# Operands of a merged projection built earlier, a gate scale moved, DMAs of two chains pinned to source order, and a reordered tail

## The chip, the cores and the metric

The kernel runs on one core of one Trainium2 chip. The metric is the time of one execution on the device in microseconds (us), the median of three runs. All arithmetic is in fp32; products on TensorE take operands that are split into a high part (fp32r) and the rest.

## The reference

One layer of an encoder is applied to two groups of 512 tokens (`g` = 0 and 1) with shared weights, model width 1024:

```python
h = rmsnorm(x, g_mix); u = h @ w_in
qk, v, o, gates, c_q, c_kv, k_r, gm = split(u)
# A: bidirectional mLSTM, 4 heads (conv + silu on qk, exponential gates, both directions added)
hm = rmsnorm(mlstm(...), g_mhead)
y_m = (sigmoid(o) * hm) @ w_mo
# B: latent attention, 8 heads, full softmax, rotary part shared
y_a = mla_attention(...) @ w_ao
g_m, g_a = sigmoid(gm)
x = x + (g_m * y_m + g_a * y_a) @ w_out
x = x + (silu(h2 @ w_gate) * (h2 @ w_up)) @ w_down      # h2 = rmsnorm(x, g_ffn)
x = x + sigmoid(x @ w_ple_gate) * (p @ w_ple)
y = rmsnorm(x, g_final)
```

## The kernel before

Activations lie transposed: a tile is 128 channels by 512 tokens of one group. `split` makes a pair of tiles for each operand: ScalarE casts the high part, VectorE subtracts it from the source for the low part. One product of two split operands is three matmuls (high by high, high by low, low by high), each 128x128 by 512 columns.

**Stages, in order.** Input norm and early projections; for each of 4 mLSTM heads its projections (`mlstm_proj`) and, for each group, `mlstm_chain`; projections of the merge gates (`merge_gate`, 16 of them, 10 before attention and the others behind attention heads 0, 1 and 3 as `BULK` says); attention, 8 heads by 2 groups, with `attn(hd, g, ...)` followed by the projections of the next head, `attn_proj(hd + 1, g, ...)`; a first chain of merged products, `w_mo` and then `w_ao`; `out_proj`; the products of the per-layer embedding (`emb`); a second chain of merged products, gate and up, then down; the gated embedding and the final norm.

**Merged products.** `chain` works through "quads". A quad covers two output column blocks by both token groups, and does with seven products (`P1`, `P2`, `P7`, `P6`, `P5`, `Q4`, `P3`) what would take eight. With an inner width of 4 tiles a product is 12 matmuls. The operand side of a quad is `Ops`: from four raw quarters, a and b (first half of the channels of group 0 and 1) and c and d (second half), it makes sums and splits them. `P1` is a, `P2` is c, `P7` is b-d, `P6` is b-d-a, `P5` is a-b, `Q4` is b-d-a+c, `P3` is d. One set of operands serves four quads. The weight side is `Seven`: when it is made it loads two 512 KB weight tiles (`wst`; two slots in the pool WP and two in WX, so two quads at a time), and before each product GpSimd adds blocks of them (for `P7`, `P6` and `P3`) and the result is split into one of five buffers `wp`. `chain` writes the products of neighbouring quads interleaved: `P6` of quad q, `P1` of q+1, `P5` of q, `P2` of q+1, `Q4` of q, `P7` of q+1, `P3` of q. Before a product it asks for the operands of that one and the next four (`need`), and makes the `Seven` of the next product's quad.

**What sets the order.** Each engine runs its queue in order. The queues are made by a scheduler with a timing model: an instruction may be moved ahead of others of its engine if the model finds it ready, and the program's order is only the priority. `tc.keep_in_program_order(r)` ties an instruction behind the one traced just before it on its engine. While `pinned[0]` is true, instructions of VectorE, ScalarE, TensorE and GpSimd are so tied (in `emb` and in the tail). DMAs, all issued from SyncE's queue (SP), are never tied before the change.

**The steps around the change.**

- mLSTM: `to` is tanh(o/2); at the end of `mlstm_chain` `zt = (to + 1) * hm` is stored to `hzd`. The factor `hg` (half of `g_mhead`, one column of 128 values for each block) is applied later in `hraw`, when the 16 tiles of `hzd` are loaded as raw quarters of `w_mo`'s operands.
- In attention head 7 (`hd == AH - 1`), the pool QL is closed, X2 (16 tiles) is opened, and `hops.need` is asked for `P1`, `P2` and `P7`, which loads all of `hzd`. `H` holds 32 tiles "h"; they hold the normalised input until the last merge gate, behind head 3.
- In the first chain, outputs of `w_mo` go through `put_z` (load a gate tile from `tmd`, multiply, store to `z1d`), those of `w_ao` through `put_y` (load from `z1d` and `tad`).
- In the second chain, the last output of each up quad makes GpSimd compute four sums and stores seven tiles to `actd`; the down quads load them back (`Loaded`).
- `emb` makes 16 products of 6 matmuls with four weight blocks `wple`, each split when its first product comes.
- The tail (pinned) works on the last two columns of group 1 in halves of 256 tokens, then sums squares, takes the inverse root, spreads it over partitions and writes the outputs (`finish`).

Of the kernel before, what the change touches and what calls it, by code (L numbers as in the profile page):

```python
# [15 lines left out]
P = 128  # L16
# [46 lines left out]
def encoder_kernel(ctx: ExitStack, tc: tile.TileContext, a):  # L63
# [3 lines left out]
    class Engine:  # L67
# [5 lines left out]
        def __getattr__(self, name):  # L73
            f = getattr(self.e, name)

            def call(*args, **kw):
                r = f(*args, **kw)  # L77
                if pinned[0]:
                    tc.keep_in_program_order(r)
                return r  # L80

            return call

    V, S, E, GP = (Engine(e) for e in (nc.vector, nc.scalar, nc.tensor, nc.gpsimd))

# [49 lines left out]
    nc.sync.dma_start(cols, a["cols"])  # L135
# [25 lines left out]
    def weight(src):  # L161
        n = src.shape[-1]
        st = WP("wst", "wst", F32, (P, 1024))
        nc.sync.dma_start(st[:, :n], src)
# [140 lines left out]
    for k in range(KD):  # L305
        nc.sync.dma_start(xs[0][k], a["x0"][k])
        if k == 0:
            wg = w8("gate")
    nc.sync.dma_start(ident, a["ident"])
# [9 lines left out]
    for k in range(KD):  # L319
        nc.sync.dma_start(xs[1][k], a["x1"][k])  # L320
# [15 lines left out]
    for g in range(G):  # L336
        s = EV("ch", "gsb")
        V.tensor_tensor(out=s, in0=early["gate", g], in1=rs1[g], op=ALU.mult)
        S.activation(out=s, in_=s, func=AF.Identity, bias=col("b_gate"))
        for d in range(2):  # L340
            for i in range(2):
                lo = 64 + 32 * i + 4 * d
                nc.sync.dma_start(rid[i][8 * d + 4 * g : 8 * d + 4 * g + 4], s[lo : lo + 4])
        nc.sync.dma_start(gsd[g], s[0:64])
# [15 lines left out]
    nc.sync.dma_start(esel, a["esel"])  # L360

    masks = []
    for d in range(2):
        st = R("tr", "mst")
        nc.sync.dma_start(st[:, 0:P], a["mask"][d])
# [11 lines left out]
    nc.sync.dma_start(lf, rid[1].rearrange("r (c t) -> (r c) t", c=8))  # L377
# [12 lines left out]
    nc.sync.dma_start(lfd.rearrange("r (c t) -> (r c) t", c=8), lf)  # L390
# [3 lines left out]
    for t, r in ((ri_n, rid[0]), (rf_n, lfd)):  # L394
        GP.memset(t, 0.0)
        for d in range(2):
            nc.sync.dma_start(t[32 * d : 32 * d + 8], r[8 * d : 8 * d + 8])
# [64 lines left out]
    def mlstm_proj(hd):  # L462
# [59 lines left out]
        for c in range(2):  # L522
            w = w8(f"o{2 * hd + c}")
            for g in range(G):
                to[g][c] = hproj(w, g, M1("to", "to"))
                S.activation(out=to[g][c], in_=to[g][c], func=AF.Tanh, scale=0.5)
        mst[hd] = (sts, va, to)

    def mlstm_chain(hd, g):
# [67 lines left out]
        for c in range(2):  # L597
# [4 lines left out]
            V.scalar_tensor_tensor(out=zt, in0=to[g][c], scalar=1.0, in1=tp, op0=ALU.add, op1=ALU.mult)  # L602
            nc.sync.dma_start(hzd[g][2 * hd + c], zt)
# [36 lines left out]
    def merge_gate(name, dst, c):  # L640
        w = w8(f"{name}{c}")
        for g in range(G):
            t = hproj(w, g, EV("bk", "tg"))
            S.activation(out=t, in_=t, func=AF.Tanh, scale=0.5)
            nc.sync.dma_start(dst[g][c], t)
# [20 lines left out]
    for half in range(2):  # L666
        whi, wlo = weight(a["wv"][half])
        for g in range(G):
            for i in range(NB):
# [9 lines left out]
                nc.sync.dma_start(vd[g][half][i], t)  # L679
    ozd = [[dr.tile([P, T], F32, name=f"ozd{g}_{c}") for c in range(AH)] for g in range(G)]  # L680
    cos = Q.pool.tile([P, T], F32, name="cos")
    nc.sync.dma_start(cos, a["cos"])
    sin = Q.pool.tile([P, T], F32, name="sin")
    nc.sync.dma_start(sin, a["sin"])
# [15 lines left out]
    for g in range(G):  # L700
        gs = Q("tr", "gs")
        nc.sync.dma_start(gs[0:64], gsd[g])
# [11 lines left out]
    def attn_proj(hd, g, wa):  # L714
# [13 lines left out]
        nc.sync.dma_start(vt.rearrange("p (a b) -> p a b", a=NB), vd[g][hd // 4].rearrange("a p c -> p a c")[:, :, c : c + P])  # L728
# [3 lines left out]
    def attn(hd, g, ops):  # L732
# [36 lines left out]
        nc.sync.dma_start(ozd[g][hd], o)  # L769

    def load(src, sl=EV, tag="bk", n="ld"):
        t = sl(tag, n)
        nc.sync.dma_start(t, src)
# [10 lines left out]
    class Ops:  # L784
# [12 lines left out]
        def part(self, name, k):  # L797
# [3 lines left out]
            if name == "P7":  # L801
                t = self.t[k] = self.tmp()
# [38 lines left out]
    class Seven:  # L841


        def __init__(self, srcs, kh, ops, out):
            n = kh * P
            st = []
            for sl, src in zip((WP, WX), srcs):
                t = sl("wst", "wst", F32, (P, 1024))
                nc.sync.dma_start(t[:, : 2 * n], src)
                st += [t[:, 0:n], t[:, n : 2 * n]]  # L850
            self.st, self.n, self.kh, self.ops, self.out = st, n, kh, ops, out
            self.bk = {}
# [23 lines left out]
        def product(self, name):  # L876
# [7 lines left out]
            for k in range(self.kh):  # L884
# [51 lines left out]
    def load4(src):  # L936
        t = ev4("ld")
        nc.sync.dma_start(t, src)
# [15 lines left out]
    for hd in range(AH):  # L954
        if hd < AH - 1:
            wa = weight(a["wa"][hd + 1])
        else:
            QL.close()
            X2 = Slots("X2", "right", x=16)
            for n in ("P1", "P2", "P7"):  # L960
                hops.need(n)
        for g in range(G):
            attn(hd, g, ops[g])
            if hd < AH - 1:
                ops[g] = attn_proj(hd + 1, g, wa)
        for _ in range(BULK[2 + hd]):
# [10 lines left out]
    def put_z(c):  # L977
        def put(at, t):
# [3 lines left out]
            nc.sync.dma_start(z1d[g][cc], m)  # L982
# [72 lines left out]
    for c in range(KD):  # L1055
# [9 lines left out]
        if c == 5:  # L1065
            st = [sl_("wst", "wst", F32, (P, 1024)) for sl_ in (WX, WX)]
            for i in range(2):
                nc.sync.dma_start(st[i], a["wple"][i])
# [7 lines left out]
    def emb(n):  # L1076
        for _ in range(n):
            c, g = todo.pop(0)
            if c // 2 == len(wple):
# [4 lines left out]
            nc.sync.dma_start(emd[g][c], t)  # L1084
# [29 lines left out]
    def gate_up(f1, f2):  # L1114
# [6 lines left out]
        def up(at, t):  # L1121
# [3 lines left out]
            if len(ac) == 4:  # L1125
# [6 lines left out]
                for n, t_ in zip(NAMES, (a_, c_, t3, t2, t1, t4, d_)):  # L1132
                    actd[f1, n] = dr.tile([P, T], F32, name=nm("actd"))
                    nc.sync.dma_start(actd[f1, n], t_)
# [70 lines left out]
    def halves(c):  # L1205
        st = (WP, WX)[c % 2]("wst", "wst", F32, (P, 1024))
        nc.sync.dma_start(st, a["w8"][W8[f"pg{c}"]])
# [23 lines left out]
    def finish(g, cs, b0=0, nb=NB):  # L1231
# [3 lines left out]
        for c0 in range(cs[0], cs[-1] + 1, per):  # L1235
# [7 lines left out]
            nc.sync.dma_start(  # L1243
# [65 lines left out]
LEAD = 2  # L1309
LATN = (3, 0)  # L1310
# [94 lines left out]
```

## Time and profile before

| | |
|---|---|
| median of 3 runs | 1937.29 us (1936.48 to 1938.13) |
| profiled execution, its own time | 1939.74 us |
| its span in the profile | 1938.0 us |
| mean granted TensorE clock in it | 0.981 |
| TensorE matmul busy | 1861.9 us, 96% |
| VectorE busy | 1260.3 us, 65% |
| ScalarE busy | 874.7 us, 45% |
| GpSimd busy | 474.4 us, 24% |
| moved by DMA | 203.40 MB, mean 105 GB/s |

Engines in the profile: PE is TensorE's matmul, PEld its weight load, DVE VectorE, ACT ScalarE, POOL GpSimd, SP the queue of DMA issues. Times are from the start of the span. A row of the timeline reads: start, duration, engine, line, operation, tile written <- tiles read, form, count, and in brackets the idle time of the engine before it with what ended it. The wrapper around the engines records every operation, so all of them carry its line (L77), and they are told apart by their tiles: `b` and `mm` are products, `wp` weight splits, `xh` and `xl` the two parts of an operand of a merged product, `sc`, `pt` and `av` the three steps of attention. A row of the windows view reads: stretch, its length, busy time and count of PE, PEld, DVE, ACT and POOL, granted clock, DMA share, GB/s.

### The profile page before, as it was taken

The numbers are of one execution on the slowest core, as the hardware profiler recorded it, in microseconds if no ns is written. First come the engines' busy times: TensorE is split into PE (matmuls) and PEld (weight loads), VectorE is DVE, ScalarE is ACT, GpSimd is POOL, SyncE is SP. The second block draws the span as 40 slices with busy tenths as digits, with TensorE's granted clock in tenths as the row PEclk, the third lists the DMA queues.
The fourth block names the chain that finished last, engine by engine and source line by source line (L and its number), as shares of the span: only waits on it lengthen the run. The fifth ranks groups of instructions, "written<-read, shape, count | busy, mean of one in ns | idle before, by whom it ended". The sixth has DMA issues, their size and how long they took to land. (4 is left out here: it accounts for less than half of the span.)

```text
span 1938.0 us, 24531 instructions
## 1 busy us (share of the span) xinstructions
PE 1861.9 (96%) x8836; PEld 1542.6 (80%) x8836; DVE 1260.3 (65%) x2135; ACT 874.7 (45%) x1711; POOL 474.4 (24%) x349
## 2 busy tenths in 40 slices
PE   7999999999999999979899989999999999999997
PEld 6888898988888888758777867777887777788886
DVE  7657575746455676878996667445444458778757
ACT  5245454535354566784533435233333344434442
POOL 3000000100000001234630014565466654232100
PEclk9999999999999999989999989999999999999998
DMA  4110112012262122137554331233223346534232
GB/s 161 50 44 33 55 35 64 34 60 82 82 202 90 55 74 73 53 115 239 163 200 153 109 114 66 87 111 106 94 97 102 115 135 218 163 120 142 87 125 87
DMA packets 95578, 203.40 MB, mean 105 GB/s; under 512 B 10400, under 2 KB 21024, under 8 KB 95456
## 3 DMA queue, kind: packets, MB, share of 16 engines
q1 hardware_dynamic: 95456, 201.83, 31.2%
q8 instruction: 69, 1.13, 0.2%
q14 instruction: 53, 0.43, 0.1%
HBM read 147.69 MB, written 54.10 MB: 104 GB/s over the span
## 5 line engine op out<-in xcount | busy, mean ns | idle before, releaser
L77 PE MATMUL b<-xh,wp 128*128 128x512 f32 x2296 | 723.4, 396 | 17.9 <-ACT wp L77 8.3
L77 PEld LDWEIGHTS b<-xh,wp 128*128 128x128 f32 x2296 | 434.5, 190 | 124.4 <-ACT wp L77 11.7
L77 PE MATMUL b<-xl,wp 128*128 128x512 f32 x1148 | 452.4, 394 | 5.9 <-DVE xl L77 5.7
L77 DVE TENSOR_TENSOR wp<-wst,wp 128x512 fp32r<-128x512 f32 (+1 forms) x284 | 271.9, 964 | 108.8 <-ACT wp L77 108.0
L77 ACT CAST wp<-wst 128x512 fp32r<-128x512 f32 (+1 forms) x284 | 171.0, 611 | 345.4 <-PE b L77 228.1
L77 PEld LDWEIGHTS b<-xl,wp 128*128 128x128 f32 x1148 | 217.8, 190 | 54.3 <-DVE xl L77 7.6
L77 PE MATMUL mm<-hh,whi 128*128 128x512 f32 x592 | 233.1, 394 | 7.2 <-ACT whi L77 7.0
L77 PE MATMUL mm<-hh,wlo 128*128 128x512 f32 x592 | 232.4, 394 | 2.2 <-DVE wlo L77 2.2
L77 PE MATMUL mm<-hl,whi 128*128 128x512 f32 x592 | 233.0, 394 | 1.1 <-DVE hl L77 1.1
L77 POOL TENSOR_TENSOR s<-wst,wst 128x512 f32<-128x512 f32 (+1 forms) x42 | 61.6, 1466 | 449.5 <-DMA wst<-w 323.4
L77 PEld LDWEIGHTS mm<-hh,whi 128*128 128x128 f32 x592 | 112.2, 190 | 30.6 <-ACT whi L77 7.0
L77 POOL TENSOR_TENSOR wst<-wst 128x512 f32<-128x512 f32 (+1 forms) x84 | 125.7, 1496 | 35.3 <-DVE wp L77 30.7
L77 PEld LDWEIGHTS mm<-hh,wlo 128*128 128x128 f32 x592 | 112.1, 189 | 26.1 <-DVE wlo L77 3.4
L77 PEld LDWEIGHTS mm<-hl,whi 128*128 128x128 f32 x592 | 112.1, 189 | 25.5 <-DVE hl L77 2.3
L77 DVE TENSOR_TENSOR u<-b,u 128x512 f32<-128x512 f32 x90 | 61.3, 687 | 107.6 <-PE b L77 82.7
L77 ACT CAST whi<-wst 128x1024 fp32r<-128x1024 f32 (+1 forms) x71 | 73.1, 1029 | 110.4 <-PE mm L77 77.6
L77 DVE TENSOR_TENSOR wlo<-wst,whi 128x1024 fp32r<-128x1024 f32 (+1 forms) x71 | 86.0, 1211 | 28.7 <-ACT whi L77 28.3
L77 POOL TENSOR_TENSOR vnl<-avt,vnh 128x512 fp32r<-128x512 f32 x16 | 21.5, 1345 | 317.6 <-ACT vnh L77 284.6
L77 DVE TENSOR_TENSOR xl<-ld,xh 128x512 fp32r<-128x512 f32 x109 | 88.7, 846 | 8.1 <-ACT xh L77 7.8
L77 PE MATMUL mm<-xh,wp 128*128 128x512 f32 (+1 forms) x288 | 81.7, 368 | 0.0
L77 ACT COPY u<-b 128x512 f32<-128x512 f32 x90 | 50.9, 586 | 66.6 <-PE b L77 65.6
L77 DVE TENSOR_TENSOR x<-x,b 128x512 f32<-128x512 f32 x84 | 56.9, 682 | 32.8 <-PE b L77 32.4
(269 smaller groups left out, 3379.4 us busy)
## 6 DMA issues: line engine op xcount, KB each, us to landing
wst<-w SPq DMA_DIRECT2D x135, 512.0 KB
ld<-actd SPq DMA_DIRECT2D x77, 256.0 KB
actd<-t SPq DMA_DIRECT2D x44, 256.0 KB
actd<-sg SPq DMA_DIRECT2D x33, 256.0 KB
x<-x SPq DMA_DIRECT2D x32, 256.0 KB
wst<-wd SPq DMA_DIRECT2D x16, 512.0 KB
hzd<-hz SPq DMA_DIRECT2D x16, 256.0 KB
tmd<-tg SPq DMA_DIRECT2D x16, 256.0 KB
```

The lines of the kernel that those rows point to most:

```text
L77: r = f(*args, **kw)
```

## The change

1. **Gate scale.** `to` becomes `hg * tanh + hg` with one more ScalarE operation for each of 16 tiles in `mlstm_proj`; the product at the end of `mlstm_chain` loses its `+ 1`, and `hraw` loses its 16 scaling operations.
2. **Operands earlier.** For heads 4 and 5 (`HOPS`), behind each of the four (head, group) steps, one of the four k of `P1`, `P2`, `P7` and `P6` is built: 4 loads into a small stage of 4 tiles, 4 splits, one subtraction on VectorE and one on GpSimd, both in place. At head 7 nothing is built; the raw quarters are forgotten, and `P5`, `Q4` and `P3` load all 16 quarters again, into X2, inside the chain. `Q4` is made from the quarters with two subtractions where there was one addition.
3. **Queue.** Inside `chain`, each DMA is tied behind the one traced before it. The `Seven` of quads 0 and 1 is made right at their first product; that of quad q+2 right behind the matmuls of `P3` of quad q and ahead of its outputs (the `hook`).
4. **`emb`.** A block of `wple` is split one block (four products) ahead.
5. **Tail.** The last column of the last half (`embed(KD - 1, ...)`) is moved ahead of two of the four output tiles of the first half, its square is kept apart (`keep=True`, so the sum takes two operands), and the other outputs are spread over the waits that follow.

```diff
+    queued = [False]
+
+    def dma(out, in_):
+        r = nc.sync.dma_start(out, in_)
+        if queued[0]:
+            tc.keep_in_program_order(r)
...  (every nc.sync.dma_start becomes dma)
@@ mlstm_proj
                 S.activation(out=to[g][c], in_=to[g][c], func=AF.Tanh, scale=0.5)
+                hc = hg[:, 2 * hd + c : 2 * hd + c + 1]
+                S.activation(out=to[g][c], in_=to[g][c], func=AF.Identity, scale=hc, bias=hc)
@@ mlstm_chain
-            V.scalar_tensor_tensor(out=zt, in0=to[g][c], scalar=1.0, in1=tp, op0=ALU.add, op1=ALU.mult)
+            V.tensor_tensor(out=zt, in0=to[g][c], in1=tp, op=ALU.mult)
@@ Ops.part
-                t = self.t[k] = self.tmp()
+                t = self.t[k] = self.tmp() or self.get("b", k)
                 add(out=t, in0=self.get("b", k), in1=self.get("d", k), op=ALU.subtract)
...
-            else:
+            elif k in self.t:
                 t = self.t[k]
                 add(out=t, in0=t, in1=self.get("c", k), op=ALU.add)
+            else:
+                t = self.get("c", k)
+                add(out=t, in0=t, in1=self.get("a", k), op=ALU.subtract)
+                add(out=t, in0=t, in1=self.get("d", k), op=ALU.subtract)
@@ Seven.product
+            if name == "P3" and self.hook:
+                self.hook()
             self.out(name, self.bk)
@@ chain
+        queued[0] = True
+
+        def make(i):
+            if i < len(quads) and i not in made:
+                made[i] = quads[i][1]()
+
         for at, (q, n) in enumerate(order):
             for i, m in order[at : at + look + 1]:
                 quads[i][0].need(m)
-            for i, m in order[at : at + 2]:
-                if i not in made:
-                    made[i] = quads[i][1]()
+            make(q)
+            if n == "P3":
+                made[q].hook = lambda q=q: make(q + 2)
             made[q].product(n)
+        queued[0] = False
@@ operands of w_mo
+    stage = [(H, "rs"), (H, "rs"), (EV, "bk"), (EV, "bk")]
+    raws = [0]
+
     def hraw(g, k):
-        t = load(hzd[g][k], X2, "x")
-        S.activation(out=t, in_=t, func=AF.Copy, scale=hg[:, k : k + 1])
-        return t
-
-    tmps = [(H, "rs"), (H, "rs"), (EV, "bk"), (EV, "bk")]
-    hops = Ops(hraw, lambda: (lambda s: s[0](s[1], "t"))(tmps.pop(0)), lambda n: V if n == "P7" else GP)
+        raws[0] += 1
+        return load(hzd[g][k], *stage[raws[0] % 4])
+
+    hops = Ops(hraw, None, lambda n: V if n == "P7" else GP)
+    hops.tmp = lambda: None
@@ attention
             X2 = Slots("X2", "right", x=16)
-            for n in ("P1", "P2", "P7"):
-                hops.need(n)
+            hops.r, hops.t = {}, {}
+            hops.raw = lambda g, k: load(hzd[g][k], X2, "x")
         for g in range(G):
             attn(hd, g, ops[g])
             if hd < AH - 1:
                 ops[g] = attn_proj(hd + 1, g, wa)
+            if hd in HOPS:
+                for n in ("P1", "P2", "P7", "P6"):
+                    hops.need(n, [2 * HOPS.index(hd) + g])
@@ emb
-            if c // 2 == len(wple):
+            while len(wple) < min(4, c // 2 + 2):
@@ tail
-    finish(1, [0, 1, 2, 3], 0, H0)
-    embed(KD - 1, 1, bk[3], toks[1], bps[1])
+    first = rs2[1]
+    finish(1, [0, 1], 0, H0)
+    embed(KD - 1, 1, bk[3], toks[1], bps[1], True)
+    finish(1, [2, 3], 0, H0)
     sums(1, H0, H0)
     inv(1, H0)
-    rs_ = rs2[1]
+    finish(1, [4, 5], 0, H0)
     spread3(1, H0, H0)
-    rs2[1], rs_ = rs_, rs2[1]
-    finish(1, [4, 5, 6, 7], 0, H0)
-    rs2[1] = rs_
+    rs2[1], second = first, rs2[1]
+    finish(1, [6, 7], 0, H0)
+    rs2[1] = second
...
+HOPS = (4, 5)
```

More of the change, by code (lines that the diff above doesn't have):

```diff
@@ L134, in encoder_kernel @@
     cols = cp.tile([P, NCOL], F32, name="cols")
-    nc.sync.dma_start(cols, a["cols"])
+    dma(cols, a["cols"])
     ident = cp.tile([P, P], F32, name="ident")
@@ L701, in encoder_kernel @@
         gs = Q("tr", "gs")
[L702 removed]
+        dma(gs[0:64], gsd[g])
         r = rope(gs, 2)
@@ L768, in attn @@
         S.copy(o, ob)
-        nc.sync.dma_start(ozd[g][hd], o)
+        dma(ozd[g][hd], o)
     def load(src, sl=EV, tag="bk", n="ld"):
         t = sl(tag, n)
-        nc.sync.dma_start(t, src)
+        dma(t, src)
         return t
@@ L981, in put @@
             V.scalar_tensor_tensor(out=m, in0=m, scalar=1.0, in1=t, op0=ALU.add, op1=ALU.mult)
-            nc.sync.dma_start(z1d[g][cc], m)
+            dma(z1d[g][cc], m)
         return put
@@ L1083, in emb @@
             S.copy(t, proj1(wple[c // 2], pp[g], 2, (c % 2) * 256))
-            nc.sync.dma_start(emd[g][c], t)
+            dma(emd[g][c], t)
     emb(2)
@@ L1133, in up @@
                     actd[f1, n] = dr.tile([P, T], F32, name=nm("actd"))
-                    nc.sync.dma_start(actd[f1, n], t_)
+                    dma(actd[f1, n], t_)
         def make(kind, put):
```

51 lines of the change are left out of this document (26 added, 25 removed).

## The prediction

> **What bounds the kernel now.** I read the page first (shares of the engines, slices), then the waits of PE, then the windows view over those stretches where PE is not full, and last the timelines of SP, ACT and PE at the places that the change touches.
>
> ```profile
> PE 1861.9 (96%) x8836; PEld 1542.6 (80%) x8836; DVE 1260.3 (65%) x2135; ACT 874.7 (45%) x1711; POOL 474.4 (24%) x349
> PE   7999999999999999979899989999999999999997
> PEclk9999999999999999989999989999999999999998
> ```
>
> PE is the bound nearly everywhere. What a change can win lies in the few slices that show 7 or 8, and these are also the ones where the granted clock falls. The waits of PE say who ends the larger stalls:
>
> ```profile
> PE sc L77 <- ACT p L77: 9.8, 4, 3.6
> PE b L77 <- ACT wp L77: 8.3, 4, 4.5
> PE b L77 <- DVE xl L77: 5.7, 3, 5.3
> ```
>
> The first is attention (`sc`), the second late weights of merged products, the third late operands of merged products. By stage:
>
> ```profile
> 100.00:540.00 440.00, 439.65 (x2563) 389.35 (x2562) 267.39 (x609) 211.37 (x519) 17.35 (x30) 1.00 0.17 57
> ...
> 756.00:785.40 29.40, 29.32 (x149) 23.75 (x147) 22.91 (x50) 22.19 (x47) 8.71 (x7) 1.00 0.16 54
> 785.40:814.10 28.70, 26.19 (x129) 20.97 (x128) 24.72 (x55) 21.39 (x44) 5.45 (x5) 1.00 0.18 56
> 814.10:839.00 24.90, 24.72 (x126) 20.46 (x124) 17.88 (x42) 21.49 (x47) 4.70 (x4) 1.00 0.44 153
> 839.00:871.50 32.50, 18.34 (x64) 13.19 (x65) 24.62 (x42) 26.21 (x52) 11.84 (x8) 0.74 0.18 62
> 871.50:900.00 28.50, 28.50 (x127) 23.42 (x126) 23.96 (x29) 14.53 (x27) 13.52 (x9) 1.00 0.88 294
> ...
> 1133.00:1144.00 11.00, 10.70 (x54) 8.40 (x52) 4.89 (x15) 5.08 (x9) 1.30 (x1) 1.00 0.54 193
> 1144.00:1166.00 22.00, 16.03 (x49) 11.78 (x49) 20.35 (x28) 12.44 (x23) 8.83 (x6) 0.77 0.33 120
> ```
>
> The mLSTM (first row) leaves PE no idle time. Heads 4, 5, 6 and 7 are the next four rows: the last one issues 64 PE instructions in 32.5 us where head 6 issues 126 in 24.9. The first merged chain starts full (127 in 28.5 us, so 0.224 us for one matmul and 2.7 us for a product of 12). `emb` loses half of its second stretch.
>
> **The price of a stall** is more than its length:
>
> ```profile
> 964.62 0.80 PE L77 MATMUL b<-xl,wp 128*128 128x512 f32 x1 [5.34 <-DVE xl L77]
> ...
> 962.70:969.70 7.00, 5.08 (x12) 4.07 (x13) 7.00 (x7) 3.28 (x6) 6.92 (x5) 0.51 0.62 198
> ...
> 1231.02 0.50 PE L77 MATMUL b<-xh,wp 128*128 128x512 f32 x1 [1.92 <-ACT wp L77]
> ...
> 1232.00:1236.00 4.00, 3.75 (x9) 2.95 (x10) 3.57 (x4) 1.11 (x2) 3.23 (x3) 0.57 0.00 0
> ```
>
> A 5.34 us stall was followed by 5.1 us at a clock of 0.51, 12 matmuls in place of 23: 2.5 us more. A stall of 1.92 us cost a stretch at 0.57 too, some 1.7 us more. I add 2.5 and 1.7. [...]
>
> **Part 1 and 2a, head 7.** What stands there now:
>
> ```profile
> L77 ACT ACTIVATE ld<-ld,hg 128x512 f32<-128x512 f32 x16 | 11.5, 753 | 0.0
> L77 ACT CAST xh<-ld 128x512 fp32r<-128x512 f32 x8 | 4.9, 649 | 0.0
> ...
> L77 DVE TENSOR_TENSOR xl<-t,xh 128x512 fp32r<-128x512 f32 x8 | 8.5, 1084 | 2.4 <-ACT xh L77 2.3
> L77 DVE TENSOR_TENSOR xl<-ld,xh 128x512 fp32r<-128x512 f32 x8 | 5.8, 740 | 1.4 <-ACT xh L77 1.3
> ```
>
> These lie ahead of attention's own casts and exponentials on ACT (26.2 busy of 32.5). At head 6's rate (24.9/126 = 0.198 us) 64 instructions take 12.7 us, so 19.8 are lost. The change takes all of it away. The 16 scalings go to the mLSTM: 16 x 0.75 = 12 us of ACT where it has 211 of 440 busy and PE waits for nothing; without that cover they would cost up to 12. I take 0.
>
> The 16 splits, 4 subtractions on DVE and 4 on POOL go to heads 4 and 5. There DVE has 22.9 + 24.7 = 47.6 us busy in 58.1, and gets 16 x 0.74 + 4 x 0.69 = 14.6: 62.2, over the span. ACT gets 16 x 0.65 = 10.4 onto 43.6 and stays below. Head 6 has 7 us of DVE to spare, into which the last quarter can slide. So heads 4 and 5 turn from PE-bound to DVE-bound, at about +4. Head 7 alone, with no projections to lay beside its softmax, keeps some loss; the row nearest to it is head 5's (129 instructions, 25.5 at 0.198, in 28.7: 3.2), and I take 4. Heads: -19.8 + 4 + 4 = -12. Ends: -18 (nothing lost in 4 and 5) and -3 (stalls there that bring the half clock along).
>
> **Part 2b and 3a, the opening of the first chain.** This is the dear part.
>
> ```profile
> 777.79 0.33 SPq L849 DMA_DIRECT2D wst<-w  x1
> ...
> 871.36 0.40 PE L77 MATMUL b<-xh,wp 128*128 128x512 f32 x1
> ...
> 871.56 0.59 ACT L77 COPY oz<-av 128x512 f32<-128x512 f32 x1 [1.20 <-PE av L77]
> ...
> 872.44 0.38 SPq L769 DMA_DIRECT2D ozd<-oz  x1
> ...
> 907.68 0.38 SPq L849 DMA_DIRECT2D wst<-w  x1
> ...
> 911.12 0.62 ACT L77 CAST wp<-wst 128x512 fp32r<-128x512 f32 x1 [0.51 <-DMA wst<-w]
> ```
>
> Now the last weight tile of quads 0 and 1 is loaded 90 us ahead (777.79), and the first merged matmul (871.36) follows the last of attention without a gap. Tied to source order, that load stands behind the store of the last head, which waits for the last `av` matmul. PE has nothing else left. The gap: copy 0.59, store issued 0.38, load to cast 911.12 - 907.68 = 3.44, cast 0.62: 5.0, with the clock 7.5.
>
> Then `P1` of quad 1. Ahead of its load SP has eight reloads for `P5`, a gate tile, the first `z1d` store, and eight reloads for `Q4`. The store can go once `P2` is out and multiplied: 5.0 + 2.5 + 2 x 2.7 + about 1.4 = 14.3 us after attention. Eight reloads are 2.1 MB, at 294 GB/s (windows row) 7.1 us, then 0.5 MB (1.8), about 1 to start and the cast: 24.8. `P1` is due at 7.5 + 4 x 2.7 = 18.3: 6.5 late. Sum 14. Ends: 7.5 (the scheduler lays `P5` and `P3` of quad 0 into that hole) and 22: `Q4` now has eight POOL additions, and beside POOL a DVE split took 1.08 in place of 0.74, so that `Q4` of quad 0 is late next. [...]
>
> **Part 3b, the rest of the first chain.** Weights of quads 2 to 5 stand behind the `z1d` store of `Q4` two products before.
>
> ```profile
> 909.96 1.29 DVE L77 TENSOR_TENSOR u<-b,u 128x512 f32<-128x512 f32 x2 [3.71 <-PE b L77]
> ...
> 914.68 1.52 SPq L982 DMA_DIRECT2D z1d<-ld  x2
> ```
>
> Two outputs taken from PSUM at 909.96 were stored 4.7 and 5.9 us later. The load has to go 3.44 + 0.62 = 4.1 us ahead of `P1`, which stands 5.4 us (`P3`, `P6`) behind the start of `P3`: a store later than 4.1 us after `Q4` (2.7 + 1.4) stalls PE. I take +3, one or two small stalls in four quads, since those stores were late with nothing waiting for them. Ends 0 and +22 (below).
>
> **Part 3c, gate, up and down.** Here the tie is meant to work, and a row shows what it can win:
>
> ```profile
> 1224.45 1.68 SPq L1134 DMA_DIRECT2D actd<-t  x2
> 1226.23 0.38 SPq L849 DMA_DIRECT2D wst<-w  x1
> ...
> 1230.34 0.62 ACT L77 CAST wp<-wst 128x512 fp32r<-128x512 f32 x1 [8.26 <-DMA wst<-w]
> ```
>
> A weight load stood behind `actd` stores on SP, ACT waited 8.26 us, and PE 1.92. With the hook the weights go ahead of the stores. The wait `b <- ACT wp` holds 8.3 us in four stalls, with the clock about 14. Some of them may hang on DVE's or ACT's own order: -9, ends 0 and -14. Past the hook, loads for down stand behind seven stores; other products cover them.
>
> **Part 4, `emb`, and the opening of the second chain.**
>
> ```profile
> 1145.38 0.50 PE L77 MATMUL mm<-plh,wp 128*128 128x512 f32 x1 [1.24 <-ACT wp L77]
> ...
> 1147.27 0.80 PE L77 MATMUL mm<-plh,wp 128*128 128x512 f32 x1 [1.16 <-DVE wp L77]
> ...
> 1156.36 0.50 PE L77 MATMUL mm<-plh,wp 128*128 128x512 f32 x1 [2.28 <-ACT wp L77]
> ...
> 1158.38 0.80 PE L77 MATMUL mm<-plh,wp 128*128 128x512 f32 x1 [1.29 <-DVE wp L77]
> ...
> 1165.64 1.84 SPq L1084 DMA_DIRECT2D emd<-em  x2
> ...
> 1166.19 0.39 PE L77 MATMUL b<-xh,wp 128*128 128x512 f32 x1
> ```
>
> All four stalls are the splits that now come one block ahead: 49 instructions at 0.224 are 11.0 of the 22 us: -11, ends -6 (the stalls alone) and -11. But the first weights of the next chain are then tied behind the last `emd` store, as in the first: 5.0 and the clock, +7.5, where PE now goes on at 1166.19 without a gap. Ends +5 and +9.
>
> **Part 5, the tail.**
>
> ```profile
> 1923.56 1.65 DVE L77 SCALAR_TENSOR_TENSOR o<-x,cols,rbc 128x256 f32<-128x256 f32 x4
> ```
>
> Two of these four outputs now come behind the last column (0.8) and the sum of squares on DVE (0.4) goes; two more small matmuls on PE come: -1, ends -2 and 0. The rest of the outputs stays on DVE.
>
> **The sum**: -12 + 14 + 3 - 9 - 11 + 7.5 - 1 = -8.5 against the profiled span of 1938.0: 1929.5. That execution's own time is 1939.74, 2.45 above the median of the runs, so the median becomes 1937.29 - 8.5 = 1928.8.
>
> **Rivals.**
> - *Slower: `z1d` stores hold the weights.* Place: quads 2 to 5 of the first chain. With a store 8 us after `Q4` each load is 3.9 late, with the clock 5.6, four times: 22 in place of 3, and 1928.8 + 19 = 1948. It decides from a total of 15, a store some 6 us late. For it: the 5.9 above. Against: DVE put splits ahead of those multiplications because nothing waited.
> - *Heads 4 and 5 do not absorb.* Three steps in four stall long enough for the half clock: heads -3 in place of -12, 1937.8. For it: DVE at 62 of 58. Against: the work is spread over four steps and free to slide.
> - *The tie does not do what it says.* The late `wp` casts stay, because ACT's order has them behind other waits: 0 in place of -9, 1937.8. For it: 8.26 us is one wait of an in-order queue. Against: a DMA ended it.
>
> **How the numbers follow.** No change is within 0.2%, 3.9 us. Chances: the forecast 0.50 (its own range 1916 to 1934), slower 0.25, heads 0.15, no tie 0.10. The two middle cases fall mostly within 3.9 us of before. Faster 0.53: nearly all of the first and a part of the last two; same 0.21; slower 0.26. The range, 1909 to 1946, takes the good ends of heads and queue together below and most of the slower rival above.
>
> **What would show it.** No `ld<-ld,hg` on ACT, and head 7 near 17 us; DVE near full between 756 and 815; a PE gap of about 5 us ended by an ACT `wp` cast at the start of each chain, clock 0.5 behind it; the second stall some 18 us later; no stall in `emb`; `b <- ACT wp` in gate and up gone. Wrong it goes if `P1` of quads 2 to 5 waits (slower), or if the scheduler fills the opening's holes (faster than forecast).

## The result: 3.4% slower, and the profile after

The changed kernel takes 2002.2 us (median of four runs, 2001.33 to 2009.04) against 1937.64 of the kernel before (four runs): ratio 1.0342, interval 1.0319 to 1.0365, 65 us slower. The forecast was 1928.8, with a range up to 1946. The profiled execution took 2009.04 us, 6.8 above the median, with a span of 2007.3, 69.3 longer than that of before; so the stages below add up to some 5 us more than the medians differ by. From the page of the changed kernel:

```profile
PE 1881.6 (94%) x8840; PEld 1553.4 (77%) x8840; DVE 1262.8 (63%) x2134; ACT 878.4 (44%) x1711; POOL 479.6 (24%) x353
PE   7999999999999998968799988998999999999997
```

TensorE has the same work and a new hole near the middle. The windows view cut at the stages (first merged chain; up to the end of `emb`; opening and length of the second chain; tail) says where. Columns: stretch, its length, busy time and count of PE, PEld, DVE, ACT and POOL, granted clock, DMA share, GB/s. First the kernel before, then the changed one:

```profile
871.30:1036.40 165.10, 157.86 (x674) 127.38 (x674) 142.21 (x174) 70.61 (x126) 71.99 (x42) 0.98 0.58 195
1036.40:1166.10 129.70, 120.49 (x513) 97.07 (x512) 84.66 (x131) 53.74 (x85) 10.22 (x7) 0.95 0.35 120
1166.10:1830.50 664.40, 647.87 (x2774) 523.41 (x2773) 405.65 (x504) 255.05 (x451) 314.86 (x211) 0.99 0.36 118
1830.50:1938.00 107.50, 93.89 (x465) 79.08 (x464) 65.17 (x134) 34.02 (x62) 0.00 (x0) 0.94 0.31 103
```

```profile
861.50:1080.10 218.60, 176.31 (x673) 136.26 (x673) 151.64 (x178) 74.65 (x131) 88.27 (x56) 0.88 0.51 176
1080.10:1198.60 118.50, 115.40 (x513) 94.31 (x512) 74.98 (x120) 47.55 (x74) 0.00 (x0) 0.99 0.33 114
1198.60:1901.30 702.70, 656.13 (x2773) 530.19 (x2773) 417.37 (x515) 260.80 (x461) 327.48 (x217) 0.97 0.34 115
1901.30:2007.00 105.70, 94.06 (x469) 79.19 (x467) 64.69 (x133) 34.01 (x62) 0.00 (x0) 0.95 0.32 105
```

| stage | forecast | measured |
|---|---|---|
| up to the end of attention (871.3 to 861.5) | -12 | -9.8 |
| first chain with its opening | +17 | +53.5 |
| `out_proj`, `emb` | -11 | -11.2 |
| second chain with its opening | -9 + 7.5 = -1.5 | +38.3 |
| tail | -1 | -1.8 |

The time up to the end of attention, `emb` and the tail came out as forecast; both chains did not. The waits of PE, first over the first chain, then over gate and up (what PE waited for: us in total, times, longest):

```profile
PE b L900 <- ACT wp L850: 25.8, 6, 7.6
PE b L900 <- ACT u L940: 7.3, 7, 2.3
...
PE b L900 <- ACT wp L850: 27.5, 9, 3.6
```

`b <- ACT wp` is the wait for late weights that the change was to remove. It is 25.8 of the 42.2 us that PE waits in the first chain (13.2 of them in its opening), and all that PE waits for in gate and up. The timeline of the first chain, for one of these stalls (SP, DVE, ACT, PE in turn):

```profile
906.83 0.33 SPq L89 DMA_DIRECT2D z1d<-ld  x1
907.20 0.43 SPq L89 DMA_DIRECT2D ld<-tmd  x1
910.85 0.32 SPq L89 DMA_DIRECT2D z1d<-ld  x1
911.21 0.43 SPq L89 DMA_DIRECT2D ld<-tmd  x1
914.86 0.32 SPq L89 DMA_DIRECT2D z1d<-ld  x1
915.29 0.86 SPq L89 DMA_DIRECT2D wst<-w  x2
...
910.13 0.69 DVE L1008 SCALAR_TENSOR_TENSOR ld<-ld,u 128x512 f32<-128x512 f32 x1 [2.12 <-DMA ld<-tmd]
...
919.25 1.66 ACT L850 CAST wp<-wst 128x512 fp32r<-128x512 f32 x3 [4.55 <-DMA wst<-w]
...
919.92 0.50 PE L900 MATMUL b<-xh,wp 128*128 128x512 f32 x1 [2.10 <-ACT wp L850]
```

One output after another goes round SP: load of its gate tile, 2.9 us until VectorE has it, multiplication, store, and only then the next gate load: 4.0 us from store to store. The two weight loads stand behind the third of these stores, and PE waits for them. In gate and up (POOL, SP, ACT, PE in turn):

```profile
1337.60 1.29 POOL L875 TENSOR_TENSOR s<-wst,wst 128x512 f32<-128x512 f32 x1 [14.29 <-DMA wst<-w]
...
1349.87 1.83 POOL L1150 TENSOR_TENSOR sg<-sg,u 128x512 f32<-128x512 f32 x1
...
1351.72 0.33 SPq L89 DMA_DIRECT2D actd<-sg  x1
1352.10 2.02 SPq L89 DMA_DIRECT2D actd<-t  x4
1354.16 0.65 SPq L89 DMA_DIRECT2D actd<-sg  x1
1354.90 1.28 SPq L89 DMA_DIRECT2D wst<-w  x2
...
1359.43 0.62 ACT L850 CAST wp<-wst 128x512 fp32r<-128x512 f32 x1 [9.61 <-DMA wst<-w]
...
1360.10 0.80 PE L900 MATMUL b<-xh,wp 128*128 128x512 f32 x1 [3.24 <-ACT wp L850]
```

The `actd` store at 1351.72 waits for GpSimd's product at 1349.87 (done 1351.70). Five stores follow, then the weights of the next gate quad, whose `P1` stalls 3.24 us. GpSimd is late because it stood 14.29 us at a weight addition ahead of that product in its own queue; the weights that it added had been issued at 1331.92, just after VectorE finished a split (1331.89), which I read as a wait for their buffer. This comes once per pair of quads, nine times.

### The profile page after: what moved, and what is told of

Read it like the earlier page. It is cut to its first block, busy times and chain, and to the rows that moved or that the text cites. A ratio compares the mean times of both kernels' runs of the same rounds, so it can differ in the third digit from the quotient of the medians.

```text
span 2007.3 us, 24437 instructions
## 1 busy us (share of the span) xinstructions
PE 1881.6 (94%) x8840; PEld 1553.4 (77%) x8840; DVE 1262.8 (63%) x2134; ACT 878.4 (44%) x1711; POOL 479.6 (24%) x353
## 4 chain that ended last, share of the span: by engine, by line
PE 66%; DMA 9%; DVE 8%; POOL 6%; issue 4%; ACT 4%; SPq 2%; DVEq 0%; ACTq 0%; POOLq 0%
PE mm L190 7%; PE mm L188 7%; PE b L900 7%; PE mm L189 7%; PE b L901 7%; PE b L902 7%; DMA wst<-w 5%; PE nm L587 3%; SPq L89 2%; PE mm L79 2%; PE mm L502 2%; PE mm L504 2%; PE mm L503 1%; DVE xl L159 1%; DVE wp L159 1%
## 5 line engine op out<-in xcount | busy, mean ns | idle before, releaser
L900 PE MATMUL b<-xh,wp 128*128 128x512 f32 x1148 | 462.1, 407 | 79.4 <-ACT wp L850 63.2
L901 PE MATMUL b<-xl,wp 128*128 128x512 f32 x1148 | 463.2, 403 | 4.9 <-DVE xl L159 4.9
L902 PE MATMUL b<-xh,wp 128*128 128x512 f32 x1148 | 449.9, 401 | 4.6 <-DVE wp L159 4.6
L159 DVE TENSOR_TENSOR wp<-wst,wp 128x512 fp32r<-128x512 f32 (+1 forms) x271 | 259.3, 968 | 187.1 <-ACT wp L850 186.6
L900 PEld LDWEIGHTS b<-xh,wp 128*128 128x128 f32 x1148 | 223.8, 195 | 142.8 <-ACT wp L850 73.2
L850 ACT CAST wp<-wst 128x512 fp32r<-128x512 f32 (+1 forms) x271 | 162.0, 611 | 387.4 <-PE b L902 192.7
L902 PEld LDWEIGHTS b<-xh,wp 128*128 128x128 f32 x1148 | 222.9, 194 | 57.2 <-DVE wp L159 7.8
L901 PEld LDWEIGHTS b<-xl,wp 128*128 128x128 f32 x1148 | 224.0, 195 | 55.5 <-DVE xl L159 7.6
L159 DVE TENSOR_TENSOR xl<-ld,xh 128x512 fp32r<-128x512 f32 x121 | 98.7, 840 | 28.0 <-ACT xh L834 18.4
L502 PE MATMUL mm<-whi,hh 128*128 128x256 f32 x256 | 72.3, 283 | 0.3 <-DVE cu L336 0.3
```

Of the source, the lines that this page charges most:

```text
L159: e.tensor_tensor(out=out, in0=src, in1=hi.bitcast(F32), op=ALU.subtract)
L502: E.matmul(out, hi[:, tb], whi[:, n], start=k == 0, stop=False)
L850: S.copy(hi, src)
L900: E.matmul(bk, whi[:, c], hi, start=bool(first) and k == 0, stop=False, **sk)
L901: E.matmul(bk, whi[:, c], lo, start=False, stop=False, **sk)
```

## The experiments

Times are compared by the ratio to the kernel before, run beside each on the same chip; a difference in us is the difference of the ratios times 1937.6, so it need not be that of the us column.

### Is it the tie, and in which chain?

Four kernels: no tie (`queued[0] = False` in `chain`, the hook kept); the tie in the first chain alone; in the second alone (`chain(..., tied=False)` for the other); and the queue part alone, put into the kernel before.

```diff
-        queued[0] = True
+        queued[0] = tied
```

> The changed kernel with no DMA tied in either chain; everything else of the change stays. Three theories. (T) The tie to source order holds loads behind waiting stores: both chains lose nothing, so 1937.6 - 10 (heads) - 11 (emb) - 1 (tail), with some loss from the reloads in the first chain: 1915 to 1928. (R) The 16 reloads and the eight POOL additions of Q4 cost the first chain its 54 us: it stays near 213 us long, second chain back to 664, total 1960 to 1975. (M) The weights are made too late in the program (one product's outputs ahead), tied or not: both chains stay as long, about 2000.

> The changed kernel with DMAs tied in the first chain alone. (T) The first chain keeps its 54 us over before, the second gives back 30 and its opening 8: about 1963. (R) the same 1963, with the first chain as long. (M) about 2000. This run and the one tied in the second chain alone should add up to the loss of both under (T).

> The changed kernel with DMAs tied in the second chain alone. (T) the first chain is near 165 us long again, the second keeps 30 and the opening 8: about 1955. (R) the first chain stays near 213 us, about 2000. (M) about 2000.

> The kernel before with the queue part of the change alone: DMAs tied in both chains, weights made at the hook; operands, gate scale, emb and tail as before. (T) about +54 in the first chain (less where the reloads lengthened the waits: +35 to +54), +30 in the second, +8 at its opening: 2010 to 2030. (R) the first chain has no reloads, so only the second loses: about 1975. (M) as (T).

| kernel | us | ratio | interval |
|---|---|---|---|
| no tie | 1926.07 | 0.9924 | 0.9909 to 0.9939 |
| tie in the first chain | 1974.80 | 1.0173 | 1.0158 to 1.0188 |
| tie in the second chain | 1956.72 | 1.0076 | 1.0061 to 1.0091 |
| queue part alone | 2007.91 | 1.0348 | 1.0331 to 1.0365 |

(T) is shown: each tie alone brings a part of the loss, and without a tie it is gone. Two of its four figures were missed: the queue part alone lies 2 us under its range, and the tie in the first chain was put at 1963; there the second chain keeps an opening stall of 9.8 us (`b <- ACT em`) that was expected to go with its tie. Without the tie the rest of the change makes the kernel 0.8% faster. The tie costs 48 us in the first chain and 29 in the second, 78 by sum, and 81 together: they add up. The queue part alone, without any reload, loses 67, so (R), the reloads, has at most the other 14, and only where the tie is. The untied kernel by stages, cut as above:

```profile
866.80:1031.90 165.10, 157.68 (x674) 126.73 (x674) 138.99 (x173) 70.70 (x126) 61.12 (x37) 0.98 0.56 188
1031.90:1148.40 116.50, 113.54 (x513) 93.15 (x511) 76.65 (x117) 46.28 (x71) 9.03 (x6) 1.00 0.38 127
1148.40:1817.20 668.80, 645.20 (x2773) 521.91 (x2773) 412.94 (x517) 262.29 (x463) 319.03 (x212) 0.99 0.36 119
```

The first chain is back at 165.1. All 16 reloads are still in the kernel, but ahead of the chain: without the tie they are issued from 840.64 to 848.98, in head 7. The second chain keeps a long opening, to which we come back.

### What does the tie hold back?

Both ties stay, and one suspect at a time is taken out of the way. Gate tiles one output ahead; the seven `actd` stores behind the next weights; the weights of quads 0 and 1 ahead of the first tied DMA; these three together.

```diff
@@ gates_ahead: put_z
-            m = load4(tmd[g][cc])
...
+            gate_tile(j + 1)
+            m = zt.pop(j)
@@ stores_late: up
-                    dma(actd[f1, n], t_)
+                    pend.append((actd[f1, n], t_))   # issued right behind the next Seven's loads
@@ weights_first: chain
-        queued[0] = True
...
+        make(0)
+        make(1)
+        queued[0] = True
```

> The changed kernel with both ties, but in put_z the gate tile of the next output is loaded ahead of this output's multiplication and store. (L) In source order each gate load stands behind the store before it, so load, multiplication and store follow one another, about 4 us for each output, and weights stand behind them: with loads one ahead the first chain keeps only its opening (13 us of stalls and their clock) and comes to about 185 us from 213: 1970 to 1980. (S) Stores that wait for their own product hold the weights however the gate tiles come: first chain 205 or more, 1995 to 2002.

> The changed kernel with both ties, but the seven actd stores of an up quad are issued behind the weights of the next make, one quad later, when GpSimd's sums are long done. (W) The weights stood behind stores that waited for GpSimd: the nine stalls of 2.5 to 3.6 us in gate and up go, the second chain comes from 694 to about 662, total about 1970. (B) The weights wait for their own buffers, which are freed by the last split of the quad before: the stalls stay, 1995 to 2002.

> The changed kernel with both ties, but the weights of quads 0 and 1 of each chain are asked for ahead of the first tied DMA. (L) The first chain's two opening stalls (5.6 and 7.6) and the half clock behind them go, 16 to 18 us: 1984 to 1987. In the second chain nothing, since without the tie the opening waits as long for the last copies of emb on ScalarE: if its tie was the cause there, another 8 to 11 go, 1975.

> The three edits together, both ties kept. If the tie costs only through these three places, it comes to the time without ties, 1920 to 1930. If there are further waits behind in-order loads (the reloads of Q4's and P5's quarters, say), 1935 to 1955.

| kernel | us | ratio | interval | against the changed kernel |
|---|---|---|---|---|
| gates ahead | 1995.22 | 1.0296 | 1.0272 to 1.0319 | -9 |
| `actd` stores late | 1974.79 | 1.0189 | 1.0166 to 1.0212 | -30 |
| weights first | 1985.21 | 1.0242 | 1.0212 to 1.0272 | -19 |
| all three | 1944.64 | 1.0033 | 1.0018 to 1.0047 | -60 |

(W) holds: the second chain's loss is the weights behind the `actd` stores. Over gate and up the wait for weights, 27.5 us above, is gone, and PE waits for nothing else than this:

```profile
PE b L900 <- ACT u L940: 1.6, 6, 0.3
```

The opening of the first chain was worth 19: both its stalls are gone. That of the second chain stayed, 10.0 us, ended by a copy of `emb`. (L) on the gate tiles was mostly wrong: 9 us in place of some 22 to 32, with an interval that touches that of the changed kernel, so the outcome is that of (S). The round trip was there, but in the passage from `w_mo` to `w_ao` something else held the chain. Left over against no tie: 21 us, as the second expectation for this kernel had it, and all in the first chain (188.8 us from its first to its last matmul in place of 164.8). Two candidates: the loads of `w_ao`'s quarters, which come at 931 to 951 here and at 849 to 880 in the untied kernel, or the `z1d` stores. So the loads were freed from the tie (in the kernel with all three edits), and the stores moved behind the next weights, alone and with the other two edits (the gate tiles then in their old place):

```diff
@@ operands_free: the loads of oops
+    def oraw(g, k):
+        tied, queued[0] = queued[0], False
+        t = load(ozd[g][k], X2, "x")
+        queued[0] = tied
+        return t
@@ z_late: put_z
-            dma(z1d[g][cc], m)
+            zpend.append((z1d[g][cc], m))   # issued right behind the next Seven's loads
```

> The kernel with both ties and the three mending edits, and now the 16 loads of w_ao's operand quarters (ozd) are not tied. (D) What was left of the tie's loss, 18.6 us over the untied kernel, is that in source order these loads come some 75 us later than without the tie, so that VectorE has its 28 splits to do in the last quarter of w_mo and in w_ao: with the loads free it goes, and the time is 1924 to 1930. (Q) It is the other waits of the queue (gate tiles, stores, the reloads of Q4's quarters): 1938 to 1945.

> The changed kernel with both ties; only the z1d stores of w_mo's outputs are moved, four at a time, behind the weights of the next make. (S) Weights stand behind z1d stores that wait for VectorE's multiplication, also in the passage from w_mo to w_ao, where VectorE is full and its multiplications are late: the first chain comes from 213 to 185 or less (its opening stalls stay, with the reloads), total 1970 to 1980. (V) VectorE itself, with the splits of w_ao's operands, is what is late in that passage: only the 2 us stalls of quads 2 and 3 go, 1990 to 1998.

> Both ties, the z1d stores and the actd stores behind the next weights, and the weights of quads 0 and 1 ahead of the first tied DMA (the gate tiles in their old place). (S) What the mended kernel still lost, 18.6 us, goes: 1922 to 1932. (V) It stays: 1940 to 1950.

| kernel | us | ratio | interval |
|---|---|---|---|
| three edits, `ozd` loads free | 1949.69 | 1.0053 | 1.0038 to 1.0067 |
| changed kernel, `z1d` stores late | 1979.56 | 1.0214 | 1.0188 to 1.0240 |
| `z1d` and `actd` stores late, weights first | 1932.08 | 0.9958 | 0.9941 to 0.9976 |

(D) falls: with the loads at 878 to 895 nothing was won, and the time lies above both expectations. (S) holds: moving the `z1d` stores is worth 25 us in the changed kernel, and 14 of the 21 that were left. The 25 are not apart from the 19 above: the second opening stall, 7.64 us at 892.49, is gone here too, since the weights of quad 1 stood behind the first of these stores. And (V) has a part: the chain takes 187 us from its first to its last matmul (213 in the changed kernel), close to the 185 that (S) named, and splits of operands on VectorE hold PE for 9.7 of them. How a store holds the weights, in the kernel with the three edits (SP, then DVE, then PE):

```profile
939.74 0.32 SPq L89 DMA_DIRECT2D z1d<-ld  x1
940.15 1.81 SPq L89 DMA_DIRECT2D ld<-ozd  x4
942.07 0.84 SPq L89 DMA_DIRECT2D wst<-w  x2
...
935.97 1.34 DVE L159 TENSOR_TENSOR xl<-ld,xh 128x512 fp32r<-128x512 f32 x2 [5.04 <-ACT xh L834]
...
939.03 0.68 DVE L1028 SCALAR_TENSOR_TENSOR ld<-ld,u 128x512 f32<-128x512 f32 x1
...
948.83 0.80 PE L900 MATMUL b<-xh,wp 128*128 128x512 f32 x1 [6.94 <-ACT wp L850]
```

VectorE stands 5.04 us at a split of `w_ao`'s operands, which waits for its cast, and has more splits to do behind it; its multiplication for the store comes at 939.03, the store at 939.74, four more operand loads behind it, and only then the weights of a quad. PE waits 6.94 us for them. With the stores behind the weights, the stalls of PE in this chain that end with a late weight cast, 9.7 us, are gone, and three that end with a split on VectorE are left (2.2, 4.7 and 1.4). What the last 7 us are was tried with one more run, below.

### The parts beside the tie

Three kernels: the kernel before with the first two parts alone; the kernel before with the hook and no tie; and the untied kernel with all of `emb` written ahead of the steps that build `P7`'s operands.

> The kernel before with the first two parts alone: the gate scale in the mLSTM, and the operands of P1, P2, P7 and P6 built in heads 4 and 5, with the reloads. Attention ended 10 us earlier in the changed kernel and 4.5 earlier in the untied one. (A) Without tied loads the scheduler brings the reloads and their splits back into head 7, so only 4 to 6 us are won: 1932 to 1935. (F) The full 10 to 12 of the forecast: 1926 to 1929.

> The kernel before with the weights made at the hook and without any tie. The untied kernel's second chain lasted 658.6 us, before 664.4. (H) That gain comes from the place of the weights in the program: 1931 to 1934. (N) It comes from what precedes the chain (emb): within 2 us of before.

> The untied kernel, with all 16 emb products and their copies written ahead of the four steps that build P7's operands of the second chain, where they stood interleaved. (C) The second chain's opening stall of 9.9 us waits for the last emb copies, pinned on ScalarE behind casts that wait for VectorE; with the copies ahead it goes with its half clock: 1926 - 10 to 12.5, 1913 to 1916. (P) P7's operands are then late instead, and PE waits for them four products later: 1921 to 1928.

Measured: 1930.16 us, 0.9958 (0.9943 to 0.9973); 1940.02, 0.9998 (0.9987 to 1.0008); 1930.29, 0.9953 (0.9940 to 0.9965).

The hook by itself does nothing, (N). The first two parts bring 8 us, between the two expectations, and not where they were looked for: attention ends 5.0 us earlier, as (A) has it, and the second chain is 4.6 shorter, for which I have no shown cause. Why only 5, where the changed kernel ended attention 10 earlier? Windows over heads 5 and 6, first of the changed kernel, then of the untied one, which ends attention as late as the kernel with these parts alone (866.8 and 866.4):

```profile
785.00:814.00 29.00, 26.99 (x129) 21.45 (x129) 27.82 (x60) 21.85 (x46) 4.25 (x3) 1.00 0.16 50
814.00:839.00 25.00, 25.00 (x129) 20.75 (x127) 16.98 (x41) 19.30 (x41) 2.58 (x2) 1.00 0.11 38
```

```profile
785.00:814.00 29.00, 25.47 (x115) 19.89 (x114) 27.60 (x54) 19.31 (x39) 7.27 (x5) 0.94 0.28 89
814.00:839.00 25.00, 23.19 (x117) 19.08 (x115) 19.22 (x46) 20.05 (x42) 5.54 (x4) 1.00 0.11 34
```

By 839 the untied kernel is 26 PE instructions behind (the kernel with these parts alone 22), at 0.2 us each some 5 us. That is ahead of the reloads, so they and their splits, which (A) named, cannot account for it. What differs there are the first weights of the chain: untied, they are loaded at 763 and 785, and their sums on GpSimd (12.8 us of work in place of 6.8) and some of their splits come into these heads; tied, none is loaded before 862.56. The queue part alone, too, ends attention 5 us earlier (866.2). So the tie keeps work of the chain out of attention, and the chain pays for it; that these sums and splits cost the 5 us was not tested by a run of its own.

The `emb` kernel tests the second chain's opening. In the untied kernel nothing is tied there, and still:

```profile
1158.36 0.80 PE L900 MATMUL b<-xh,wp 128*128 128x512 f32 x1 [9.91 <-ACT em L79]
```

With the copies moved ahead that stall is gone, but five others of 1.3 to 4.0 us (11.4 in all) come between 1164 and 1182, and some 5 us are lost: (P), a little beyond its 1928 (1930.29). As I read it, what `emb`'s stalls had covered is VectorE's and ScalarE's work on the second chain's operands; take the stalls away and that work is the next bound.

### A faster version

In the passage to `w_ao` the kernel before, the untied one and the one tied in the second chain alone have a stall of 5.3 us, ended by a split on VectorE. The untied kernel with `w_ao`'s sums on VectorE instead of GpSimd; the tie in the second chain alone with its `actd` stores late; both together; and, for the rest of the first chain's loss, both chains tied with all stores late, weights first and these sums on VectorE.

```diff
-    oops = Ops(..., lambda n: V if n == "P7" else GP)
+    oops = Ops(..., lambda n: V)
```

> The untied kernel with all sums of w_ao's operands on VectorE. In every kernel PE stalls 5.3 us (and the half clock, 2.5) in the passage to w_ao, where VectorE is full: its splits take 1.75 us beside GpSimd's sums, 0.68 alone. (P) Beside GpSimd is what costs: eight sums more on VectorE are 5.4 us, a dozen instructions at 0.68 in place of 1.75 give back 12: the stall goes, 1917 to 1921. (F) VectorE is simply full: the stall grows, 1926 to 1934.

> The tie in the second chain alone, with the actd stores behind the next weights. The chain lasted 656.4 us so in the mended kernel, against 658.6 with no tie: 1923 to 1928 if the two chains do not touch each other, 1940 or more if the second chain's tie costs in another way once the first is free.

> The untied first chain with w_ao's sums on VectorE, and the second chain tied with its actd stores behind the next weights. The two edits gave 1921.7 and 1922.9 against 1926.1 alone; they lie in different chains, so their gains of 4.4 and 3.2 should add: 1917 to 1920. If they share something, 1921 to 1924.

> Both chains tied, all stores behind the next weights, first weights ahead, and w_ao's sums on VectorE. The tied first chain was left with 8 us of stalls (2.2, 4.7 and 1.4) in the passage to w_ao, ended by splits on VectorE beside GpSimd. (P) If these are the whole rest of the tie's loss, it comes from 1932 to the best version's 1917 to 1921. (Q) If order on the queue costs apart from it, it stays at 1925 to 1932.

| kernel | us | ratio | interval |
|---|---|---|---|
| sums on VectorE | 1921.67 | 0.9903 | 0.9884 to 0.9923 |
| tie in the second chain, stores late | 1922.92 | 0.9920 | 0.9896 to 0.9943 |
| both | 1919.01 | 0.9886 | 0.9870 to 0.9903 |
| all tied and mended | 1924.86 | 0.9917 | 0.9901 to 0.9932 |

The third is 1.1% faster than the kernel before and 4.4% faster than the changed one; its interval lies clear of the untied kernel's, those of the first two do not. (P) on the sums has the trace for it: VectorE takes 1.75 us an instruction beside GpSimd's sums, and mostly 0.67 where they are its own. DVE, then POOL, in the untied kernel:

```profile
956.61 1.75 DVE L1019 TENSOR_TENSOR ld<-ld,ld 128x512 f32<-128x512 f32 x1
958.28 1.75 DVE L159 TENSOR_TENSOR xl<-t,xh 128x512 fp32r<-128x512 f32 x1
...
956.10 1.71 POOL L875 TENSOR_TENSOR s<-wst,wst 128x512 f32<-128x512 f32 x1
957.77 1.71 POOL L818 TENSOR_TENSOR ld<-ld,ld 128x512 f32<-128x512 f32 x1
```

and DVE with the sums on it, then POOL:

```profile
952.15 0.67 DVE L818 TENSOR_TENSOR ld<-ld,ld 128x512 f32<-128x512 f32 x1
...
948.66 8.93 POOL L876 TENSOR_TENSOR wst<-wst 128x512 f32<-128x512 f32 x1
```

In the untied kernel VectorE goes in step with GpSimd at 1.7 us an instruction. With the twelve sums that were GpSimd's on VectorE it mostly takes 0.67 us an instruction, and between 950 and 980 it did 43 instructions in place of 31, only five of them such sums. The stall of 5.3 us shrinks to 1.6. The price falls on GpSimd: its weight addition in the last row, 1.75 us in the untied kernel, reads 8.93 beside fourteen instructions of VectorE (the profile's spans on GpSimd are rough). Which engine gives way, and by what, no run here settles.

The last kernel falls between the two expectations: 1924.86. Of the first chain's stalls one of 5.1 us, ended by a weight split on VectorE, and one of 1.3 are left, and the chain lasts 167.3 us against 158.8 in the third kernel, from its first to its last matmul. So the tie's remainder, 6 us with intervals that just overlap, is again in that passage; which order on SP brings it about stays open.

## Why the prediction was wrong, point by point

- **Heads, -12: right in size** (-9.8), though only some 5 of it come from the operands' new place; the rest goes with the tie, which keeps work of the chain out of attention, and was paid back in the chain. Counted back from the end of attention by PE instructions, head 7 takes 15.4 us where some 17 were expected (32.7 before). Heads 4 to 6 take 7 us more than before in the changed kernel and 11 more in the one with the first two parts alone; +4 was forecast. The rival that they do not absorb the work thus has a part.
- **Opening of the first chain, +14: right in mechanism and within its ends, 5 us short.** The gap of 5.0 was 5.58, the second of 6.5 was 7.64, and taking both away gave 19. The second stall ended 31 us after attention, not 25, and ScalarE's cast of its weights (891.83) came directly behind a cast that had waited for a GpSimd sum for `Q4`, so how much of it is the load and how much that sum is not shown. The "about 1 to start" in its 24.8 was my estimate; the rows show only the whole way of a weight load from issue to cast, 3.44 us before (907.68 to 911.12) and 3.96 in the changed kernel (915.29 to 919.25).
- **Rest of the first chain, +3: the step that failed first.** It was to cost one or two small stalls, because "those stores were late with nothing waiting for them". The rival had the mechanism (a load behind a store more than some 6 us late) and 22 us; measured, with the opening's 19 taken off the 53.5, it is some 34. Two things were missing. The gate loads are tied too, so a store is not late by VectorE's order alone but by a whole load behind the store before it; taking that away gave 9. And the rival took the lateness of a kernel without the tie, while in the passage to `w_ao` VectorE is nearly full (19.3 of 20 us from 980) and stores of the changed kernel come 17 and 15 us apart (975.91, 992.63, 1007.50), with the weights of a quad behind the last.
- **Gate, up and down, -9: wrong in sign, the second failure.** "With the hook the weights go ahead of the stores" holds for the stores of the same quad. The weights of the next gate quad are made one quad later and stand behind those seven stores, which wait for GpSimd. The text saw stores ahead of loads only for down. The term should have been some +30, which the edit of the `actd` stores gave back. And the wait that it counted on winning was small: the largest of the four stalls (4.48 at 1634) stands in the untied kernel as one of 5.20.
- **`emb`, -11: right (-11.2). Opening of the second chain, +7.5: right in size** (8.46), **with half of the cause.** The wait that it names is real: where the queue part is alone and `emb` as before, PE waits 9.67 us there for the weights' cast, and not at all before. But the new `emb` brings the stall without any tie (9.91 us, ended by its last copy), and with the weights ahead of the tie it is 10.0. The forecast has no term for that.
- **Tail, -1: right** (-1.8; -0.9 untied, 106.6 us).
- **Range.** Both failed steps have one cause: I asked of each load which stores stand ahead of it in its own quad, but not what each of these stores waits for, and what is queued before that. With +30 for gate and up and the rival's 22, the sum would have been 1987, still 15 short.

## What to carry to other kernels

The queue in source order issued no load before the last store ahead of it had its data (behind one waiting `actd` store SP issued nothing from 1333 to 1351.72): before tying one, walk the source and write beside every load the latest producer of any store ahead of it, loads of the next iterations included. If such a queue is wanted, write the stores behind the next iteration's loads; here this edit was worth 30 us for the `actd` stores and 25 for the `z1d` stores. And with the 9.91 us stall of the second chain's opening removed, five others came, 11.4 us in all: look behind a stall that is taken away for the next bound.

## What the runs showed of the hardware

**A waiting store blocked the queue, not the transfer engines.** From 1333 to 1351.72 SP issued nothing. Up to 1336 the DMA engines were 85% busy with what had been issued before, and from there on 8% (the windows view, last but one number):

```profile
1336.00:1351.70 15.70, 15.70 (x70) 12.89 (x69) 10.41 (x11) 5.71 (x10) 14.02 (x9) 1.00 0.08 32
```

The rows of SP's queue at 907 to 915 and at 1351 to 1355 have the same order: the weights are issued behind the last store, at 915.29 behind 914.86 and at 1354.90 behind 1354.16.

**The price of a short stall was not fixed by its length.** Windows of 4 us behind stalls of 1.86, 3.24, 3.33 and 3.41 us in the changed kernel (the clock is the third number from the end):

```profile
942.20:946.20 4.00, 3.95 (x10) 3.06 (x11) 2.81 (x4) 1.14 (x2) 3.05 (x3) 0.57 0.41 128
1360.10:1364.10 4.00, 4.00 (x9) 3.14 (x10) 4.00 (x4) 2.00 (x4) 3.21 (x3) 0.50 0.01 2
1449.40:1453.40 4.00, 3.98 (x17) 3.21 (x18) 4.00 (x4) 2.46 (x5) 3.22 (x3) 1.00 0.02 5
1579.10:1583.10 4.00, 3.97 (x17) 3.15 (x18) 3.99 (x4) 2.41 (x5) 3.18 (x3) 1.00 0.03 9
```

Behind a stall of 1.86 us the clock was 0.57, behind one of 3.24 it was 0.50, behind those of 3.33 and 3.41 it was 1.00. My flat 1.7 us for a short stall is therefore a mean at best. What decides between the two, no run here shows.
